# Hybrid encoder layer on one core: the scans of each second head pair and the additions of weight blocks in DRAM placed behind the products of v and z_a, and two of eight pairs of k-tiles, not three, taken as seven products

## The chip, the core and the metric

The kernel runs on one core of a Trainium2 chip. The core has five engines that run side by side, each with its own queue of instructions in a fixed order: PE (matmuls; PEld is its loading of weights), DVE and ACT (elementwise work), POOL (elementwise work, and the DMAs that add) and SP (all other DMAs). The metric is the device time of one execution, in microseconds (us); lower is better.

## The reference

One encoder layer on x of 256 tokens by 2048. After an RMS norm one projection of 2048 x 18432 gives nine blocks of 2048 columns. Five of them (q, v, two forget gates, z_a) feed group A: 16 heads of a gated linear recurrence in chunks of 64 tokens, run forward and backward, summed, normed by head and gated by silu(z_a). The other four feed a short convolution. Both results go through an output projection of 4096 x 2048; an embedding gate and a last norm follow.

```python
hn = _rmsnorm(h, norm_w[i])
proj = hn @ w_in[i]
q, v, f_fwd, f_bwd, z_a, b_gate, c_gate, h_b, z_b = jnp.split(proj, IN_SPLITS, axis=-1)
o_a = _hgrn2_bidirectional(jax.nn.silu(q), v, f_fwd, f_bwd, lb_all[:, i])
o_a = _head_rmsnorm(o_a, hgrn_norm_w[i]) * jax.nn.silu(z_a)
```

Within a chunk the recurrence needs the running sum of log f along the tokens: these running sums are the scans that the change moves.

## The kernel before, in words

**Precision.** Every fp32 weight tile is split into a rounded high part and a low remainder: `Stream.split` casts on ACT (L101) and subtracts on DVE (L102), from `raw` (three buffers of 1 MB, loaded by SP) into `spl` (five buffers). x is split the same way into `xs`. A product of two split matrices is three matmuls (`three`, L523 to L525), or a wide one and a short one where x stands on the right (`gemm_part`, L403 and L401). `Stream.get` keeps the splits three parts ahead of PE.

**Groups.** `two_pairs(i)` handles two head pairs, i and i+1, for i = 0, 2, 4, 6. Each group has two stages. First come the projections: for each of the two pairs, three calls of `gemm_in` (forget forward, forget backward, q), 96 steps of k-tiles in all. Then v and z_a for both pairs at once: `gemm_two` in group 0 and `gemm_vz` in groups 2, 4 and 6. Four convolution projections per channel group follow after the last group, and the output projection after these.

**Seven products.** `gemm_vz` goes through eight pairs of k-tiles (`half`). A plain pair takes eight block products of three matmuls each, 24 matmuls. For a pair in `VZ_SUMS` the 2 x 2 x 2 block product is done with seven products instead of eight, 21 matmuls, at the price of sums: sums of x blocks (`xsums`, once, in group 2, into `xsum`) and sums of weight blocks. The latter are made in DRAM: `prepare` copies two blocks of weights into a tile `vz` (L306, SP), `add_up` adds to them with accumulating DMAs on POOL's queue in three steps (step 0 at L314, steps 1 and 2 at L318), and the result is loaded like a weight tile (`raw<-vz`, L76). A pair with sums splits 3.5 parts, a plain one 2. The banks of the seven products, `ex`, `ey` and two that the scores use as well, are emptied after the last pair with sums (L445 to L449).

**Mixing.** `mix_forgets` (gates, logarithms) and `mix_pair` (scans at L652 and L656, exponentials, the factors `kc`, `qc` and `kx` on POOL at L687 and L693) prepare a pair; `scores` multiplies them on PE (L706, L750), and `outputs` multiplies with v.

**What sets the order.** A counter `tick` runs along with the k-steps of PE. `at(dt, fn)` records the instructions of `fn` when the counter is dt further. A scheduler then places each engine's instructions by its own forecast of readiness; `high_priority` moves an instruction ahead by an offset, and `tc.keep_in_program_order` holds an instruction behind what its engine has been given before. `gemm_vz` counts 49 ticks before the change and 46 after, so a group has 145 or 142. In group 0 the additions come at ticks 98 to 112, during `gemm_two`; in groups 2 and 4 they are for the next group.

Of the kernel before, what the change touches and what calls it, by code (L numbers as in the profile page):

```python
# [12 lines left out]
ALU = mybir.AluOpType  # L13
# [6 lines left out]
T = 256  # L20
# [95 lines left out]
def tile_hymba_encoder(  # L116
# [15 lines left out]
    act, dve, pool, pe = nc.scalar, nc.vector, nc.gpsimd, nc.tensor  # L132
# [16 lines left out]
    ws = Stream(tc, rawp, splp, 3)  # L149


    VZ_ORDER, VZ_SUMS = (0, 1, 2, 3, 4, 6, 5, 7), (2, 4, 6)
    dramp = ctx.enter_context(tc.tile_pool(name="dramp", bufs=1, space=bass.MemoryType.DRAM))
    vz_prepared = {}
    blocks = {}
# [96 lines left out]
    smask = early[:, 0:T]  # L252
# [5 lines left out]
    for j in range(4):  # L258
        sgn = 1 if j < 2 else -1
        pool.affine_select(  # L260
            out=tri[:, j, :], in_=tri[:, j, :], compare_op=ALU.is_ge, fill=0.0, base=0,
# [35 lines left out]
    def at(dt, fn):  # L297
        pend.append((now[0] + dt, len(pend), fn))
# [109 lines left out]
    def gemm_in(c, i, orders={}):  # L408

        acc = acc_in(c, i)  # L410
        for g in range(4):
            gemm_part(acc, ws.get(blocks[c, i][g]), g, orders=orders)
        return acc
# [41 lines left out]
                for m in range(2):  # L455
                    act.activation(dst[:, m], dst[:, m], AF.Copy, scale=rx[:, m : m + 1])

    def evac(acc, dst, tmpp):

        with tc.high_priority(offset=200):  # L460
            for m in range(2):
                r = tmpp.tile([P, T], F32, tag="r", name="r", bufs=2)
                act.copy(out=r, in_=acc[m][:, 1, :])  # L463
                dve.tensor_tensor(out=dst(m), in0=acc[m][:, 0, :], in1=r, op=ALU.add)  # L464
# [8 lines left out]
    acc3 = [acc_in(c, 0) for c in first[:2]]  # L473
# [22 lines left out]
    ap_ = actx.enter_context(tc.tile_pool(name="ap", bufs=1, side="right"))  # L496
# [143 lines left out]
                in1=mixa[:, hd, 0, :], op0=ALU.mult, op1=ALU.subtract,  # L640
            )

    def mix_pair(i, xf, qt, lf):


        pf = ap_.tile([P, 2, 2, T], F32, tag="pf", name=f"pf{i}")
        dd = ap_.tile([P, 2, 2, T], F32, tag="dd", name=f"dd{i}")
        pv = [pf[:, d] for d in range(2)]
        dv = [dd[:, d] for d in range(2)]
        lfl = lf.rearrange("p a b c -> p (a b c)")  # L650
        for h in range(2):
            dve.tensor_tensor_scan(  # L652
                out=pv[0][:, h, :], data0=smask, data1=lf[:, 0, h, :], initial=0.0, op0=ALU.mult, op1=ALU.add
            )
            o = (2 + h) * T - 1
            dve.tensor_tensor_scan(  # L656
                out=pv[1][:, h, :], data0=lfl[:, o : o + T], data1=smask, initial=0.0, op0=ALU.add, op1=ALU.mult
            )
        pf4, pb4, df4, db4 = c64(pv[0]), c64(pv[1]), c64(dv[0]), c64(dv[1])
        lb4 = c64(lf[:, 1])  # L660
        for h in range(2):
            dve.tensor_tensor(
                out=df4[:, h], in0=pf4[:, h], in1=pf4[:, h, :, 31:32].broadcast_to([P, 4, CH]), op=ALU.subtract
# [119 lines left out]
    def two_pairs(i):  # L783
        vt = ap_.tile([P, 2, 512], F32, tag="vt", name=f"vt{i}")
        zt = ap_.tile([P, 2, 512], F32, tag="zt", name=f"zt{i}")
        ss = ap_.tile([P, 2, 2, 2], F32, tag="ss", name=f"ss{i}", bufs=2)
        ogs, steps, forgets = [], [], []
        before = last_two[0]
        if i == 6:
            for z in range(4):  # L790
                at(10 + 10 * z, lambda z=z: prepare(prepared[z]))
        else:


            todo = vz_prepared[i + 2]
            for z, what in enumerate(todo):
                at(50 + 10 * z, lambda what=what: prepare(what))
                for step in range(3):
                    dt = (126 + 10 * z, 160 + 4 * z, 174 + 4 * z)[step] if i else 98 + 6 * step + z
                    at(dt, lambda what=what, step=step: add_up(what, step))  # L800
        if i == 2:

            def xsums(z):
                k = 2 * VZ_SUMS[z]
                a, t = xq[1][:, 0].rearrange("p (k t) -> p k t", k=2), xq[1][:, 1].rearrange("p (o t) -> p o t", o=4)
                act_sums(xs[:, k : k + 2], a, t)
                act_split(xq[0][:, z], xs[:, k : k + 2], t)

            for z in range(len(VZ_SUMS)):
                at(10 + 12 * z, lambda z=z: xsums(z))  # L810
        for e in range(2):
            xf = ap_.tile([P, 2, 2, T], F32, tag="xf", name=f"xf{i + e}", bufs=2)
            qt = ap_.tile([P, 2, T], F32, tag="qt", name=f"qt{i + e}")
            first3 = i + e == 0

            kicks = {(0, 1): ({}, ONE, BOTH), (2, 0): (ONE, BOTH, {}), (4, 0): ({}, {}, BOTH), (6, 0): ({}, {}, BOTH)}
            kick = kicks.get((i, e), ({}, {}, BOTH if i + e else {}))
            for j, (c, dst) in enumerate(((B_FF, xf[:, 0]), (B_FB, xf[:, 1]), (B_Q, qt))):
                evac(acc3[j] if first3 else gemm_in(c, i + e, kick[j]), lambda m, dst=dst: dst[:, m, :], ap_)

            def mix(e=e, xf=xf, qt=qt):
                forgets.append((xf, qt, mix_forgets(i + e, xf, qt)))
                if e == 0:
                    if before:
                        before()
                    steps.append(mix_pair(i, *forgets[0]))

            if first3:

                at(15, mix)  # L830
            else:
                mix()

        def out(e):
            ogs.append(ap_.tile([P, 2, 2, P], F32, tag="ogz", name=f"ogz{i + e}", bufs=2))
            steps[e][1](vt, ogs[e], ss[:, e])

        if i == 0:

            at(18, lambda: steps[0][0]())  # L840
            at(19, lambda: steps.append(mix_pair(i + 1, *forgets[1])))
            at(46, lambda: out(0))
            at(46, lambda: steps[1][0]())
            at(60, lambda: out(1))
            gemm_two(B_V, i, vt)
            xctx.close()
            xqp = xqctx.enter_context(tc.tile_pool(name="xqp", bufs=1, side="left", reuse_waits="tile"))
            xq.append(xqp.tile([P, len(VZ_SUMS), 4, 2, P], F32R, name="xsum"))
            xq.append(xqp.tile([P, 2, 512], F32, name="xd"))
            gemm_two(B_ZA, i, zt)  # L850
        else:

            at(4, lambda: steps[0][0]())
            gemm_vz(i, vt, zt)
            at(8, lambda: steps.append(mix_pair(i + 1, *forgets[1])))
            at(12, lambda: out(0))
            at(32, lambda: steps[1][0]())
            at(42, lambda: out(1))

        def rest():  # L860
            gate_two(i, zt)
            if i < 6:
                at(24, lambda: finish_two(ogs, ss, zt, ogs))
                for e in range(2):
                    at(32, lambda e=e: turn(i + e, ogs[e], "yx"[e]))
            else:

                def keep():
                    kept.extend(psm.tile([P, 2, 2, P], F32, tag=f"sc{e}", name=f"kept{e}") for e in range(2))
                    finish_two(ogs, ss, zt, kept)  # L870

                at(50, keep)

        last_two[0] = rest
# [360 lines left out]
```

## Time and profile before

| | us |
|---|---|
| median of 3 runs | 1152.24 |
| lowest and highest | 1151.96, 1156.35 |
| the profiled execution | 1151.24 |
| its span, first to last instruction | 1149.5 |

The mean granted clock of TensorE is 0.992. Of the profiled time 1.7 us lie around the span. A line of the profile names engine, source line, operation, the tile written and the tiles read. "Idle before, releaser" is how long the engine stood and what let it go on. Windows give the busy time of each engine in a stretch. The matmuls of a row overlap their neighbours, so their pitch, start to start, says what one costs, and not its duration.

### The profile page before, as it was taken

The numbers are of one execution on the slowest core, as the hardware profiler recorded it, in microseconds if no ns is written. First come the engines' busy times: TensorE is split into PE (matmuls) and PEld (weight loads), VectorE is DVE, ScalarE is ACT, GpSimd is POOL, SyncE is SP. The second block draws the span as 40 slices with busy tenths as digits, with TensorE's granted clock in tenths as the row PEclk, the third lists the DMA queues.
The fourth block names the chain that finished last, engine by engine and source line by source line (L and its number), as shares of the span: only waits on it lengthen the run. The fifth ranks groups of instructions, "written<-read, shape, count | busy, mean of one in ns | idle before, by whom it ended". The sixth has DMA issues, their size and how long they took to land.

```text
span 1149.5 us, 17024 instructions
## 1 busy us (share of the span) xinstructions
PE 1114.5 (97%) x6455; PEld 950.8 (83%) x6455; DVE 829.3 (72%) x1100; ACT 677.6 (59%) x947; POOL 300.3 (26%) x251
## 2 busy tenths in 40 slices
PE   9999999789996999999999999999999999999996
PEld 8888888668884888778888888888888888888886
DVE  7899477765784767976657776774767879878573
ACT  6786568445974568755644544544546665565563
POOL 1135324601263016403323413323423000000011
PEclk9999999989999999999999999999999999999999
DMA  9776994997659965487899998999998988887531
GB/s 352 269 251 216 243 298 166 201 288 242 199 156 253 341 212 174 149 277 212 234 302 276 267 297 267 261 295 292 278 257 249 355 278 288 306 295 268 202 128 74
DMA packets 86082, 286.42 MB, mean 249 GB/s; under 512 B 8304, under 2 KB 29424, under 8 KB 67312
## 3 DMA queue, kind: packets, MB, share of 16 engines
q1 hardware_dynamic: 69264, 258.76, 64.6%
q0 software_dynamic: 16448, 26.22, 15.2%
q8 instruction: 51, 0.84, 0.3%
q10 hardware_dynamic: 288, 0.34, 0.1%
q14 instruction: 31, 0.25, 0.1%
HBM read 283.20 MB, written 54.53 MB: 294 GB/s over the span
## 4 chain that ended last, share of the span: by engine, by line
PE 70%; DVE 11%; DMA 6%; POOL 6%; ACT 4%; issue 2%; SPq 0%; DVEq 0%; ACTq 0%; POOLq 0%
PE a L403 28%; PE a L401 14%; DVE spl L102 4%; DMA raw<-in_w_in_dram 4%; PE pg L996 3%; PE pg L997 3%; PE pg L995 3%; DMA raw<-vz 2%; PE pa L523 2%; PE pa L524 2%; PE pa L525 2%; ACT spl L101 2%; POOL kc L687 2%; DVE pf L652 1%; POOL qc L687 1%
## 5 line engine op out<-in xcount | busy, mean ns | idle before, releaser
L102 DVE TENSOR_TENSOR spl<-raw,spl 128x1024 fp32r<-128x1024 f32 (+2 forms) x419 | 503.7, 1215 | 225.9 <-ACT spl L101 223.1
L403 PE MATMUL a<-xs,spl 128*128 128x512 f32 x1792 | 622.8, 393 | 0.4 <-DVE xs L344 0.2
L101 ACT CAST spl<-raw 128x1024 fp32r<-128x1024 f32 (+2 forms) x419 | 413.1, 998 | 263.1 <-PE a L401 89.2
L401 PE MATMUL a<-xs,spl 128*128 128x256 f32 x1792 | 496.3, 279 | 0.0
L403 PEld LDWEIGHTS a<-xs,spl 128*128 128x128 f32 x1792 | 334.3, 187 | 74.8 <-issue 0.6
L401 PEld LDWEIGHTS a<-xs,spl 128*128 128x128 f32 x1792 | 337.4, 189 | 2.1
L1112 POOL TENSOR_TENSOR hh<-hh,fw 128x512 f32<-128x512 f32 (+1 forms) x9 | 11.0, 1226 | 250.7 <-ACT gt L1111 248.1
L463 ACT COPY r<-a 128x256 f32<-128x256 f32 x112 | 40.3, 367 | 37.9 <-PE a L401 37.7
L524 PE MATMUL avz<-spl,xs 128*128 128x512 f32 x138 | 55.4, 401 | 4.9 <-DVE spl L102 4.8
L523 PE MATMUL avz<-spl,xs 128*128 128x512 f32 x138 | 55.3, 401 | 1.2 <-DVE qt L464 1.2
L525 PE MATMUL avz<-spl,xs 128*128 128x512 f32 x138 | 54.5, 395 | 0.0
L995 PE MATMUL pg<-spl,ht 128*128 128x512 f32 (+1 forms) x120 | 45.2, 377 | 0.0
L996 PE MATMUL pg<-spl,ht 128*128 128x512 f32 (+1 forms) x120 | 45.1, 376 | 0.0
L997 PE MATMUL pg<-spl,ht 128*128 128x512 f32 (+1 forms) x120 | 45.0, 375 | 0.0
L755 POOL TENSOR_TENSOR s<-early 128x256 f32<-128x256 f32 x16 | 16.3, 1028 | 105.4 <-DVE early L754 105.4
L101 ACT CAST spl<-early 128x1024 fp32r<-128x1024 f32 (+1 forms) x29 | 28.7, 990 | 19.0 <-PE pb_y L525 7.5
L102 DVE TENSOR_TENSOR spl<-early,spl 128x1024 fp32r<-128x1024 f32 (+1 forms) x29 | 32.8, 1147 | 9.6 <-ACT spl L101 9.1
L468 POOL TENSOR_TENSOR xf<-xf,rbc 128x1024 f32<-128x1024 f32 x8 | 20.8, 2602 | 68.7 <-DVE rbc L379 49.3
L524 PEld LDWEIGHTS avz<-spl,xs 128*128 128x128 f32 x138 | 26.5, 192 | 12.8 <-DVE spl L102 7.5
L912 POOL TENSOR_TENSOR cg<-cg,hb 128x512 f32<-128x512 f32 x8 | 14.8, 1854 | 82.1 <-DVE hb L464 82.1
L523 PE MATMUL pa<-spl,mixa 128*128 128x512 f32 x88 | 34.5, 392 | 0.0
L525 PE MATMUL pa<-spl,mixa 128*128 128x512 f32 x88 | 34.3, 390 | 0.0
(322 smaller groups left out, 1685.5 us busy)
## 6 DMA issues: line engine op xcount, KB each, us to landing
raw<-in_w_in_dram SPq DMA_DIRECT2D x106, 1024.0 KB, 7.4
raw<-in_w_in_dram SPq DMA_DIRECT2D x82, 256.0 KB, 4.4
raw<-in_w_out_dram SPq DMA_DIRECT2D x36, 512.0 KB, 5.2
sums<-in_w_out_dram SPq DMA_DIRECT2D x32, 512.0 KB, 11.0
raw<-in_w_in_dram SPq DMA_DIRECT2D x26, 512.0 KB, 6.6
raw<-sums SPq DMA_DIRECT2D x13, 1024.0 KB, 5.5
vz<-in_w_in_dram SPq DMA_DIRECT2D x36, 256.0 KB, 6.9
raw<-vz SPq DMA_DIRECT2D x9, 1024.0 KB, 7.4
```

What stands on the lines that cost most here:

```text
L101: self.nc.scalar.copy(out=v[:, :, 0], in_=r)
L102: self.nc.vector.tensor_tensor(out=v[:, :, 1], in0=r, in1=v[:, :, 0], op=ALU.subtract)
L401: pe.matmul(a[:, :T], lhsT=lhsT, rhs=xs[:, kt, 0, :], start=False, stop=(kt == NKT - 1))
L403: pe.matmul(a, lhsT=lhsT, rhs=xs[:, kt, :, :].rearrange("p s n -> p (s n)"), start=(kt == 0), stop=False)
L463: act.copy(out=r, in_=acc[m][:, 1, :])
L523: pe.matmul(acc, lhsT=ah, rhs=w[:, 0], start=start, stop=False)
L524: pe.matmul(acc, lhsT=ah, rhs=w[:, 1], start=False, stop=False)
L525: pe.matmul(acc, lhsT=al, rhs=w[:, 0], start=False, stop=stop)
L687: pool.tensor_tensor(out=c64(dst[:, d]), in0=c64(src[:, d, :, half * P : (half + 1) * P]), in1=g.unsqueeze(3).broadcast_to([P, 2, 2, CH]), ...
L995: pe.matmul(acc[m], lhsT=lh, rhs=wh, start=(kt == 0), stop=False)
L996: pe.matmul(acc[m], lhsT=lh, rhs=wl, start=False, stop=False)
L997: pe.matmul(acc[m], lhsT=ll, rhs=wh, start=False, stop=(kt == nk - 1))
```

## The change

Five edits:

- `VZ_SUMS` goes from (2, 4, 6) to (2, 5) and the pairs run in plain order: two pairs of k-tiles with sums in each `gemm_vz`, with pairs 3 and 4 between them.
- The additions for the next group get later due times: steps at 166, 196 and 220 ticks from the start of the group, that is 24, 54 and 78 ticks into the next group's projections. Group 0 keeps its times.
- `mix_pair(i + 1)` of groups 2, 4 and 6 comes 4 ticks after `gemm_vz`, not 8, and its four scans are kept in program order.
- The eviction of the second pair's q has priority offset 500, not 200.
- `out(1)` comes at tick 46, not 42.

```diff
-    VZ_ORDER, VZ_SUMS = (0, 1, 2, 3, 4, 6, 5, 7), (2, 4, 6)
+    VZ_ORDER, VZ_SUMS = range(8), (2, 5)
...
-    def evac(acc, dst, tmpp):
+    def evac(acc, dst, tmpp, offset=200):
-        with tc.high_priority(offset=200):
+        with tc.high_priority(offset=offset):
...
-    def mix_pair(i, xf, qt, lf):
+    def mix_pair(i, xf, qt, lf, here=False):
+        place = tc.keep_in_program_order if here else lambda instr: instr
...
-            dve.tensor_tensor_scan(
-                out=pv[0][:, h, :], data0=smask, data1=lf[:, 0, h, :], initial=0.0, op0=ALU.mult, op1=ALU.add
+            place(
+                dve.tensor_tensor_scan(
+                    out=pv[0][:, h, :], data0=smask, data1=lf[:, 0, h, :], initial=0.0, op0=ALU.mult, op1=ALU.add
+                )
             )
...
-                    dt = (126 + 10 * z, 160 + 4 * z, 174 + 4 * z)[step] if i else 98 + 6 * step + z
+                    dt = (166, 196, 220)[step] + z if i else 98 + 6 * step + z
...
-                evac(acc3[j] if first3 else gemm_in(c, i + e, kick[j]), lambda m, dst=dst: dst[:, m, :], ap_)
+                acc, offset = acc3[j] if first3 else gemm_in(c, i + e, kick[j]), 500 if e and j == 2 else 200
+                evac(acc, lambda m, dst=dst: dst[:, m, :], ap_, offset)
...
-            at(8, lambda: steps.append(mix_pair(i + 1, *forgets[1])))
+            at(4, lambda: steps.append(mix_pair(i + 1, *forgets[1], here=True)))
...
-            at(42, lambda: out(1))
+            at(46, lambda: out(1))
```

What stands where on the engines follows from the scheduler. Before, DVE in group 2: the scores of pair 2 are taken over (L754), and at once, within `gemm_vz`, come the scans of pair 3 (shown as SCALAR_TENSOR_TENSOR at L652 and L656) and what is made of them, with the splits (L102) of the first pair of k-tiles with sums between and behind.

```order
L754 COPY_PREDICATED early<-early,scps_173 128x512
L754 COPY_PREDICATED early<-early,scps_174 128x512
L652 SCALAR_TENSOR_TENSOR pf_2447<-early,lf_2023 128x256
L656 SCALAR_TENSOR_TENSOR pf_2447<-lf_2023,early 128x256
L652 SCALAR_TENSOR_TENSOR pf_2447<-early,lf_2023 128x256
L656 SCALAR_TENSOR_TENSOR pf_2447<-lf_2023,early 128x256
L662 TENSOR_TENSOR dd_2448<-pf_2447 128x256
L665 TENSOR_TENSOR dd_2448<-pf_2447 128x256
L662 TENSOR_TENSOR dd_2448<-pf_2447 128x256
L102 TENSOR_TENSOR spl_2123<-raw_2045,spl_2123 128x512
L665 TENSOR_TENSOR dd_2448<-pf_2447 128x256
L671 TENSOR_TENSOR gx<-dd_2448,pf_2447 128x2x3
```

After the change, the same place (lines of the changed kernel: L759 was L754, L654 and L660 are the scans). The splits follow the scores; the scans stand after the sums that finish v and z_a (L453) and a split of the next group's weights.

```order
L759 COPY_PREDICATED early<-early,scps_170 128x512
L759 COPY_PREDICATED early<-early,scps_171 128x512
L102 TENSOR_TENSOR spl_2101<-raw_2023,spl_2101 128x512
L102 TENSOR_TENSOR spl_2118<-raw_2116,spl_2118 128x2x512
L102 TENSOR_TENSOR spl_2135<-raw_2116,spl_2135 128x2x512
...
L453 TENSOR_TENSOR zt_1353<-avz_3_2013,zt_1353 128x512
L102 TENSOR_TENSOR spl_2424<-raw_2422,spl_2424 128x4x256
L654 SCALAR_TENSOR_TENSOR pf_2391<-early,lf_2001 128x256
L660 SCALAR_TENSOR_TENSOR pf_2391<-lf_2001,early 128x256
L654 SCALAR_TENSOR_TENSOR pf_2391<-early,lf_2001 128x256
L102 TENSOR_TENSOR spl_2445<-raw_2422,spl_2445 128x4x256
```

The scans and all that hangs on them have moved out of `gemm_vz` into the next projections. On POOL, before, group 2: the additions for group 4 follow the scores' sums (L755), within `gemm_vz`; the factors of pair 3 (L687, L693) stand behind the first two additions of step 1.

```order
L755 TENSOR_TENSOR s_2104<-early 128x256 x2
L314 DMA vz_2_84<-in_w_in_dram 256x1x256
L593 TENSOR_TENSOR qt_1706<-qt_1706,sq_2020 128x512
L314 DMA vz_2_84<-in_w_in_dram 256x1x256
L314 DMA vz_4_85<-in_w_in_dram 256x1x256 x2
L314 DMA vz_6_86<-in_w_in_dram 256x1x256 x2
L318 DMA vz_2_84<-vz_2_84 128x512
L318 DMA vz_4_85<-vz_4_85 128x512
L687 TENSOR_TENSOR qc_2471<-pf_2447,ge_2457 128x256
L687 TENSOR_TENSOR kc_2470<-dd_2448,ge_2457 128x256 x2
L693 TENSOR_TENSOR kx_2476<-kc_2470,ge_2457 128x512
```

After the change, the same engine from the factors of pair 3 on (L692, L698), which is in the projections of group 4. Step 0 follows `kx` of pair 3, step 1 the sums of its scores (L760), and step 2 `kx` of pair 4, the last row of factors ahead of `gemm_vz` of group 4.

```order
L698 TENSOR_TENSOR kx_2420<-kc_2414,ge_2401 128x512
L314 DMA vz_2_83<-in_w_in_dram 256x1x256 x2
L314 DMA vz_5_84<-in_w_in_dram 256x1x256 x2
L760 TENSOR_TENSOR s_2636<-early 128x256
...
L760 TENSOR_TENSOR s_2636<-early 128x256
L318 DMA vz_2_83<-vz_2_83 128x512
L318 DMA vz_5_84<-vz_5_84 128x512
...
L698 TENSOR_TENSOR kx_2805<-kc_2799,ge_2786 128x512
L318 DMA vz_2_83<-vz_2_83 128x512
L318 DMA vz_5_84<-vz_5_84 128x512
```

The additions have left `gemm_vz` of groups 2 and 4, but step 2 now comes just ahead of the `gemm_vz` that uses its result.

More of the change, by code (lines that the diff above doesn't have):

```diff
@@ L651, in mix_pair @@
         for h in range(2):
-            dve.tensor_tensor_scan(
-                out=pv[0][:, h, :], data0=smask, data1=lf[:, 0, h, :], initial=0.0, op0=ALU.mult, op1=ALU.add
+            place(
+                dve.tensor_tensor_scan(
+                    out=pv[0][:, h, :], data0=smask, data1=lf[:, 0, h, :], initial=0.0, op0=ALU.mult, op1=ALU.add
+                )
             )
             o = (2 + h) * T - 1
-            dve.tensor_tensor_scan(
-                out=pv[1][:, h, :], data0=lfl[:, o : o + T], data1=smask, initial=0.0, op0=ALU.add, op1=ALU.mult
+            place(
+                dve.tensor_tensor_scan(
+                    out=pv[1][:, h, :], data0=lfl[:, o : o + T], data1=smask, initial=0.0, op0=ALU.add, op1=ALU.mult
+                )
             )
```

## The prediction

> **What bounds the kernel now.** I read the page's busy shares first, then the waits of PE, then windows over the stages.
>
> ```profile
> span 1149.5 us, 17024 instructions
> PE 1114.5 (97%) x6455; PEld 950.8 (83%) x6455; DVE 829.3 (72%) x1100; ACT 677.6 (59%) x947; POOL 300.3 (26%) x251
> ...
> PE ey L523 <- ACT spl L101: 9.8, 5, 3.1
> PE avz L524 <- DVE spl L102: 5.0, 6, 2.0
> PE ey L524 <- DVE spl L102: 3.8, 5, 0.8
> PE ex L524 <- DVE spl L102: 3.2, 3, 1.4
> PE avz L523 <- DVE qt L464: 1.2, 1, 1.2
> ```
>
> PE is the bound, and what it waits for (total us, times, longest) lies almost wholly in one routine: `avz`, `ex` and `ey` are written only where v and z_a are multiplied, and these rows add up to 23.0 us. The windows below hold one line per stretch: its length, then busy time of PE, PEld, DVE, ACT and POOL, the granted clock, the DMA share and GB/s. First the three products of v and z_a (groups 2, 4 and 6), then the projections ahead of the first two.
>
> ```profile
> 195.36:256.63 61.27, 50.71 (x273) 37.70 (x272) 42.57 (x52) 31.21 (x40) 20.05 (x21) 0.94 0.85 219
> 330.27:389.76 59.49, 49.65 (x273) 38.04 (x272) 40.82 (x51) 29.82 (x39) 19.10 (x21) 0.94 0.90 245
> 463.64:512.06 48.42, 45.00 (x274) 36.05 (x272) 41.61 (x51) 29.42 (x39) 13.37 (x12) 1.00 0.66 222
> ...
> 127.84:195.36 67.52, 67.52 (x394) 59.13 (x392) 45.99 (x65) 46.74 (x63) 24.53 (x15) 1.00 0.86 257
> 256.63:330.27 73.64, 73.64 (x513) 65.01 (x513) 50.13 (x73) 56.06 (x85) 23.03 (x13) 1.00 0.65 215
> ```
>
> The projections leave PE no idle time. The three products issue the same matmuls, yet take 61.27, 59.49 and 48.42 us. What the third lacks is the additions in DRAM for a next group: it is a control inside the trace. A stretch of group 4 shows what a wait does on PE (start, duration, idle before):
>
> ```profile
> 369.37 0.39 PE L524 MATMUL avz<-spl,xsum 128*128 128x512 f32 x1
> 369.59 0.39 PE L525 MATMUL avz<-spl,xsum 128*128 128x512 f32 x1
> 373.10 0.50 PE L523 MATMUL ey<-spl,xsum 128*128 128x512 f32 x1 [3.12 <-ACT spl L101]
> ...
> 375.38 0.63 PE L523 MATMUL scps<-spl,xsum 128*128 128x512 f32 x1
> 375.81 0.63 PE L524 MATMUL scps<-spl,xsum 128*128 128x512 f32 x1
> ```
>
> A matmul of 512 columns starts 0.22 to 0.23 us after the one before; after this wait of 3.12 us the pitch is 0.43. So a wait can cost more than itself, and the granted clock of 0.94 in the first two windows is the same thing.
>
> **The change part by part.**
>
> *One pair of k-tiles more as plain products.* 24 matmuls instead of 21, in three groups: 9 x 0.23 = **+2.1 us** on PE, which has no cover.
>
> *The additions move.* Before, POOL's rows of them lie inside the group's v and z_a; now the first addition stands behind `kx` of the group's second head pair and the last behind `kx` of the next group's first pair, in the projections. From the first two windows go at most (61.27 - 48.42) + (59.49 - 48.42) = **-23.9 us**, if they become like the third. The 1.2 us for `qt` are part of that: only the first window has this wait, and the new offset of 500 puts that eviction a split earlier. The additions must not hold up the projections instead. The trace has a stretch of projections with additions landing:
>
> ```profile
> 127.00:152.00 25.00, 25.00 (x144) 21.83 (x143) 12.49 (x14) 13.28 (x17) 3.26 (x4) 1.00 1.09 280
> ```
>
> DMA is at 1.09 there and PE is busy 25.00 of 25.00 us. I take 0 for the new place.
>
> *The scans move.* The third window's own idle time has two sources:
>
> ```profile
> 470.05 1.23 DVE L652 TENSOR_TENSOR_SCAN pf<-early,lf 128x256 f32<-128x256 f32 x1
> ...
> 482.43 3.63 DVE L102 TENSOR_TENSOR spl<-raw,spl 128x1024 fp32r<-128x1024 f32 x2
> ...
> 481.70 0.39 PE L523 MATMUL avz<-spl,xs 128*128 128x512 f32 x1
> 484.12 0.50 PE L524 MATMUL avz<-spl,xs 128*128 128x512 f32 x1 [2.03 <-DVE spl L102]
> ...
> 496.06 0.39 PE L525 MATMUL avz<-spl,xsum 128*128 128x512 f32 x1
> 496.88 0.50 PE L523 MATMUL ey<-spl,xsum 128*128 128x512 f32 x1 [0.43 <-ACT spl L101]
> 498.14 0.50 PE L524 MATMUL ey<-spl,xsum 128*128 128x512 f32 x1 [0.76 <-DVE spl L102]
> ```
>
> From 470.05 to 482.43 DVE works off the second head pair's mixing, and a split that PE wants comes late: start to start 2.42 us instead of 0.23. Then two pairs of k-tiles with sums follow each other (4, 6), and ACT and DVE fall behind: (0.82 - 0.23) + (1.26 - 0.23) = 1.6 us. The scans now stand behind v and z_a, and pairs 2 and 5 are never neighbours. Together 2.2 + 1.6 = 3.8 us. I take 3.0 of it as gone, since splits still share DVE with scores and evictions; the same order stands in all three windows, so 3 x 3.0 = **-9.0 us** (between 0 and -11.4).
>
> *What is late next: the second head pair's scores.* Its scans, and all its mixing behind them, now wait for v and z_a. The third window gives the chain's length, since no addition stands in POOL's way there:
>
> ```profile
> 259.88 0.68 DVE L453 TENSOR_TENSOR zt<-avz,zt 128x512 f32<-128x512 f32 x1
> 260.48 1.21 DVE L102 TENSOR_TENSOR spl<-raw,spl 128x1024 fp32r<-128x1024 f32 x1
> ...
> 484.94 1.60 POOL L687 TENSOR_TENSOR qc<-pf,ge 128x256 f32<-128x256 f32 x1
> ...
> 280.88 0.30 PE L706 MATMUL scps<-qc,dd 128*32 128x128 f32 x2
> ...
> 315.80 5.02 POOL L687 TENSOR_TENSOR kc<-dd,ge 128x256 f32<-128x256 f32 x1 [3.65 <-DVE dd L678]
> ```
>
> From the first scan to the end of the last `qc` it is 486.54 - 470.05 = 16.5 us. The order puts the scans behind the last sum of v and z_a and one split, which end 261.69 - 256.63 = 5.1 us into the next projection. So the factors are there 21.6 us in. PE takes the scores up 280.88 - 256.63 = 24.2 us in. The slack is 2.6 us, not much for a chain over three engines: `kc` alone took 5.02 us once, against 1.60 for this `qc`. I put **+2.0 us** for the three places together (0 if the slack holds, 3 x 4 = 12 if POOL is slow each time; nearer to 0, because the measured chain ran while DVE was fuller).
>
> *What is late next: the sums.* The last addition now waits for `kx`, and the load of the sums waits for it on SP's queue, with the weight tiles queued behind it:
>
> ```profile
> 323.03 1.05 POOL L693 TENSOR_TENSOR kx<-kc,ge 128x512 f32<-128x512 f32 x1
> ...
> 327.55 0.33 SPq L76 DMA_DIRECT2D raw<-vz  x1
> ...
> 345.61 0.39 PE L523 MATMUL ey<-spl,xsum 128*128 128x512 f32 x1
> ...
> raw<-vz SPq DMA_DIRECT2D x9, 1024.0 KB, 7.4
> vz<-in_w_in_dram POOLq DMA_DIRECT2D x18, 256.0 KB, 8.5
> vz<-vz POOLq DMA_DIRECT2D x18, 256.0 KB, 9.5
> ...
> DMA to landing us min/median/max: 4.6/7.5/15.9
> ```
>
> `kx` ends at 324.08; with 9.5 us to landing (the last figure of these rows) the sums are whole at 333.6, so their load goes out 6 us later than its 327.55 and lands at 341.0. PE wants the first part of it at 345.61, a cast and a split, some 2.2 us, behind the landing: slack 2.4 us. The tile behind it has a further pair's time. **+1.0 us** for groups 4 and 6 together (0 to 2 x 4).
>
> *At nothing:* one sum's preparation less on SP and DVE in group 2 (its projections have no PE idle), 1.5 splits less per group, `out(1)` four ticks later, since no wait of PE is for it.
>
> Sum against the profiled execution: -23.9 - 9.0 + 2.1 + 2.0 + 1.0 = -27.8. Its time is 1151.24 (span 1149.5), so 1123.4; the median of the runs shown is 1.0 higher, hence **1124 us**.
>
> A rule weighs on the price of new waits. The Trainium skill, "TensorE: Matmul & The Clock Gate", Part 1, says that the clock halves after an idle window of about 3.4 us. By it three waits of 3 us would cost 9. The trace halves the pitch after 3.12 us already and keeps it so for at least 2.7 us, 1.3 us more each: 13. Both are inside my range.
>
> **The rivals.**
>
> *The contention moves along.* The additions take the same DMA time wherever they stand. Their queue took 15.2% of the span for 26.22 MB, and a group's three sums are twelve transfers of 256 KB, 3.1 MB:
>
> ```profile
> q0 software_dynamic: 16448, 26.22, 15.2%
> ```
>
> That is 174.7 x 3.1 / 26.2 = 21 us for three sums, 14 for two; with the projections' 0.65 x 73.64 = 48 us it makes 62 of 73.64, or 0.84. If a projection stalled at that, the 23.9 us would return: 1124 + 24 = 1148, within 0.5% (5.8 us, about what a measurement of this kernel can tell from no change). Against it stands the row at 1.09 without a PE wait. The Trainium skill, "Trainium Kernel Development and Optimization", Key Constraints, says that DMAs issued from SP, ACT and POOL share the same 16 engines and interleave; by that rule the move saves no DMA time, which is this rival.
>
> *The scores wait.* The slack of 2.6 us is overrun at all three places by 4 us: 1124 + 12 - 2 = 1134. For it: the `kc` of 5.02 us. Against it: that one had `gate_two` and the transposes beside it.
>
> *The sums come very late, and it ends slower.* SP stands at the load of the sums with all weight tiles behind it. To be slower by 0.5% each of two groups must lose (1158 - 1124) / 2 = 17 us beyond 2.4 us of slack: a last addition landing 29 us behind `kx`. The longest landing on these tiles is 15.9 us.
>
> *The change does nothing:* excluded for scans and additions, since the order shows both moved.
>
> **How the numbers follow.** Forecast (1115 to 1130): 0.66. Scores or sums late by some us (1130 to 1142): 0.22. Contention moved (1146 to 1158): 0.07. Slower: 0.05. With the whole 11.4 gone and no new wait the sum gives 1119; the floor of 1115 leaves 4 us below that for the scatter of the runs shown (1151.96 to 1156.35). 1138 at the top takes in most of the second case. Faster by over 0.5%: 0.66 + 0.22 = 0.88; within: 0.07; slower: 0.05.
>
> **What would show it.** Right: windows over the three products of about 46 us each at clock 1.00, no waits of PE on `ey`, PE full in the projections. Wrong: idle of PE ahead of the scores or `cx`; a late `raw<-vz` with PE waiting on `spl`; or projections longer by what the products lost.

## The result, and the profile after

| | before | after |
|---|---|---|
| median, four runs each, us | 1154.30 | 1116.69 |
| lowest and highest | 1151.96, 1157.54 | 1115.47, 1120.22 |
| the profiled execution | 1151.24 | 1116.85 |
| its span | 1149.5 | 1115.1 |

The ratio is 0.9677, with a 95% interval of 0.9641 to 0.9714: faster by 38 us by the medians and by 34 by the two profiled executions. The forecast was 1124 us, with a range of 1115 to 1138.

From the page of the changed kernel, the span and the busy shares:

```profile
span 1115.1 us, 16970 instructions
...
PE 1105.0 (99%) x6464; PEld 951.2 (85%) x6464; DVE 826.7 (74%) x1088; ACT 671.6 (60%) x939; POOL 291.5 (26%) x239
```

PE is busy 9.5 us less, although it has nine matmuls more: the matmuls that ran at half speed after a wait are gone. By the granted clock they were some 7 us of it (an estimate: 0.06 of 61.27 and of 59.49 us). The waits of PE (engine, line, waited for, total us, times, longest), all that are left:

```profile
PE wps L242 <- DVE wz L237: 1.1, 1, 1.1
PE avz L523 <- DVE qt L464: 0.6, 1, 0.6
```

Of 23.0 us of waits in v and z_a 0.6 are left, and none is on `ey` or a split. The windows of the changed kernel: v and z_a of group 2, the projections behind them, v and z_a of group 4, projections, v and z_a of group 6.

```profile
194.22:238.79 44.57, 44.57 (x276) 36.98 (x275) 33.22 (x36) 28.18 (x34) 4.54 (x4) 1.00 0.69 231
238.79:312.68 73.89, 73.89 (x514) 65.23 (x513) 58.46 (x86) 54.68 (x85) 35.99 (x26) 1.00 0.74 209
312.68:358.15 45.47, 44.84 (x276) 37.04 (x275) 33.52 (x37) 29.58 (x36) 4.54 (x4) 1.00 0.78 260
358.15:432.04 73.89, 73.89 (x514) 65.21 (x513) 58.49 (x86) 55.58 (x86) 35.93 (x26) 1.00 0.79 234
432.04:476.65 44.61, 44.61 (x276) 37.02 (x275) 33.34 (x36) 28.64 (x35) 6.01 (x7) 1.00 0.77 254
```

Read lengths first: 61.27, 59.49 and 48.42 us have become 44.57, 45.47 and 44.61, at a clock of 1.00. The two projections, which took in the additions and the scans, have PE busy in all of their 73.89 us, as before. DVE is the column that shows the move: 7 to 9 us less in a product, 8 more in the first projection. The span lost 34.4 us, and 16.7 + 14.0 + 3.8 = 34.5 of that lie in the three products. All other stretches together changed by 0.1 net.

The two new risks were the scores of the second head pair and the sums. From the timeline of the changed kernel, group 2's projections start at 238.79 (start, duration):

```profile
241.79 0.68 DVE L654 TENSOR_TENSOR_SCAN pf<-early,lf 128x256 f32<-128x256 f32 x1
242.39 0.66 DVE L660 TENSOR_TENSOR_SCAN pf<-lf,early 128x256 f32<-128x256 f32 x1
...
255.53 1.05 POOL L698 TENSOR_TENSOR kx<-kc,ge 128x512 f32<-128x512 f32 x1
256.53 4.24 POOL L314 DMA_DIRECT2D vz<-in_w_in_dram  x4
...
263.27 0.30 PE L711 MATMUL scps<-qc,dd 128*32 128x128 f32 x2
...
306.63 1.05 POOL L698 TENSOR_TENSOR kx<-kc,ge 128x512 f32<-128x512 f32 x1
307.63 1.67 POOL L318 DMA_DIRECT2D vz<-vz  x2
...
308.10 4.72 DVE L102 TENSOR_TENSOR spl<-raw,spl 128x1024 fp32r<-128x1024 f32 x1 [0.45 <-ACT spl L101]
...
308.72 3.01 POOL L468 TENSOR_TENSOR xf<-xf,rbc 128x1024 f32<-128x1024 f32 x1
...
312.93 0.33 SPq L76 DMA_DIRECT2D raw<-vz  x1
```

The scans start 3.0 us into the projection, the last factor `kx` is done at 256.58, and PE takes the scores up at 263.27: a slack of 6.7 us. The last additions of the sums are issued from 307.63, and their load goes out at 312.93, 5.3 us later. Nobody waits for it. The split on DVE that takes 4.72 us in place of 1.2 is the one cost in sight, and it comes back below.

### The profile page after: what moved, and what is told of

Read it like the earlier page. It is cut to its first block, busy times and chain, and to the rows that moved or that the text cites. A ratio compares the mean times of both kernels' runs of the same rounds, so it can differ in the third digit from the quotient of the medians.

```text
span 1115.1 us, 16970 instructions
## 1 busy us (share of the span) xinstructions
PE 1105.0 (99%) x6464; PEld 951.2 (85%) x6464; DVE 826.7 (74%) x1088; ACT 671.6 (60%) x939; POOL 291.5 (26%) x239
## 4 chain that ended last, share of the span: by engine, by line
PE 94%; ACT 2%; DMA 2%; POOL 1%; DVE 1%; issue 0%; DVEq 0%; ACTq 0%; POOLq 0%
PE a L403 34%; PE a L401 18%; PE avz L523 3%; PE avz L524 3%; PE avz L525 3%; PE pg L1004 3%; PE pg L1003 3%; PE pg L1005 3%; PE pa L523 2%; PE pa L524 2%; PE pa L525 2%; DMA raw<-in_w_in_dram 2%; PE a L424 1%; PE a L422 1%; PE a L423 1%; PE pb_sc L524 1%
## 5 line engine op out<-in xcount | busy, mean ns | idle before, releaser
L102 DVE TENSOR_TENSOR spl<-raw,spl 128x1024 fp32r<-128x1024 f32 (+2 forms) x413 | 505.7, 1238 | 190.1 <-ACT spl L101 187.5
L101 ACT CAST spl<-raw 128x1024 fp32r<-128x1024 f32 (+2 forms) x413 | 409.0, 1001 | 250.6 <-PE a L401 88.1
L523 PE MATMUL avz<-spl,xs 128*128 128x512 f32 x156 | 61.0, 391 | 0.6 <-DVE qt L464 0.6
L525 PE MATMUL avz<-spl,xs 128*128 128x512 f32 x156 | 60.7, 389 | 0.0
L524 PE MATMUL avz<-spl,xs 128*128 128x512 f32 x156 | 60.7, 389 | 0.0
L692 POOL TENSOR_TENSOR qc<-pf,ge 128x256 f32<-128x256 f32 x16 | 23.2, 1453 | 106.5 <-ACT ge L679 95.6
L468 POOL TENSOR_TENSOR xf<-xf,rbc 128x1024 f32<-128x1024 f32 x8 | 22.0, 2750 | 73.4 <-DVE rbc L379 49.4
L102 DVE TENSOR_TENSOR spl<-early,spl 128x1024 fp32r<-128x1024 f32 (+1 forms) x29 | 32.9, 1147 | 9.4 <-ACT spl L101 8.7
L523 PEld LDWEIGHTS avz<-spl,xs 128*128 128x128 f32 x156 | 29.3, 188 | 6.9 <-DVE qt L464 0.8
L523 PE MATMUL pa<-spl,mixa 128*128 128x512 f32 x88 | 34.5, 392 | 0.0
L525 PEld LDWEIGHTS avz<-spl,xs 128*128 128x128 f32 x156 | 29.3, 188 | 6.1
## 6 DMA issues: line engine op xcount, KB each, us to landing
sums<-in_w_out_dram SPq DMA_DIRECT2D x32, 512.0 KB, 11.4
```

Source lines behind the costliest of these rows:

```text
L101: self.nc.scalar.copy(out=v[:, :, 0], in_=r)
L102: self.nc.vector.tensor_tensor(out=v[:, :, 1], in0=r, in1=v[:, :, 0], op=ALU.subtract)
L523: pe.matmul(acc, lhsT=ah, rhs=w[:, 0], start=start, stop=False)
L524: pe.matmul(acc, lhsT=ah, rhs=w[:, 1], start=False, stop=False)
L525: pe.matmul(acc, lhsT=al, rhs=w[:, 0], start=False, stop=stop)
L692: pool.tensor_tensor(out=c64(dst[:, d]), in0=c64(src[:, d, :, half * P : (half + 1) * P]), in1=g.unsqueeze(3).broadcast_to([P, 2, 2, CH]), ...
```

## The experiments

Three theories stood ahead of the runs. **A**: the additions' transfers inside v and z_a are the root, as the third product, which has none, says. **B**: the scans and the late splits behind them are the root. **C**: the number of sums, or two pairs of k-tiles with sums as neighbours, is the root. Each run was timed in three rounds, beside the kernel before in the same rounds. The last column has the lengths of the three products of v and z_a in the profiled execution.

| run | what it is | us | before, us | ratio, 95% interval | products, us |
|---|---|---|---|---|---|
| e1 | before, additions at the new due times | 1150.78 | 1152.84 | 0.998 [0.9969, 0.9992] | 58.14, 57.83, 50.98 |
| e8 | before, all additions out of the products | 1147.81 | 1151.85 | 0.9965 [0.9951, 0.9979] | 50.26, 54.13, 54.69 |
| e2 | before, scans behind | 1137.85 | 1152.84 | 0.9864 [0.9838, 0.989] | 52.43, 52.88, 45.72 |
| e3 | before, two sums (2, 5) | 1131.17 | 1152.84 | 0.9807 [0.9784, 0.9831] | 52.02, 50.28, 46.97 |
| e5 | after, additions at the old due times | 1117.18 | 1152.84 | 0.9684 [0.9661, 0.9706] | 45.89, 44.57, 44.57 |
| e6 | after, scans back | 1129.33 | 1151.85 | 0.9802 [0.9782, 0.9823] | 48.54, 48.72, 48.78 |
| e7 | after, three sums in the old order | 1120.46 | 1151.85 | 0.9721 [0.9701, 0.9741] | 43.90, 49.64, 45.18 |
| e4 | after, three sums (2, 4, 6) in plain order | 1122.35 | 1151.85 | 0.9745 [0.9726, 0.9763] | 43.89, 48.18, 46.30 |
| e11 | before, additions left out | 1129.01 | 1152.47 | 0.9793 [0.9757, 0.9828] | 49.93, 47.93, 48.51 |
| e12 | e7, additions left out | 1116.35 | 1152.47 | 0.9683 [0.965, 0.9716] | 43.89, 43.90, 43.89 |
| e9 | before, three sums (2, 4, 6) in plain order | 1148.93 | 1152.47 | 0.9967 [0.9951, 0.9983] | 59.34, 56.16, 48.31 |
| e10 | before, two sums as neighbours | 1131.99 | 1152.47 | 0.982 [0.979, 0.985] | 53.00, 51.11, 46.47 |

### One part alone: e1, e8, e2, e3

The additions alone, at the due times of the change:

```diff
-                    dt = (126 + 10 * z, 160 + 4 * z, 174 + 4 * z)[step] if i else 98 + 6 * step + z
+                    dt = (166, 196, 220)[step] + z if i else 98 + 6 * step + z
```

> The kernel before with the later due times of the additions alone (three sums, old order of k-tiles, scans as before). Step 0 now stands behind kx of the second head pair, which with the scans as before still lies inside v and z_a; steps 1 and 2 are in the projections. Theory A (the DMA traffic of the additions inside v and z_a costs 23.9 us): half of the traffic is gone or more, so the windows of groups 2 and 4 fall from about 60 to 48-54 us and the time by 12 to 24 us. Theory B (the scans are the root: they delay the splits, the splits free the raw buffers late, and only then do loads and additions collide): under 8 us, windows of 57 us or more. Theory C (the number and neighbourhood of sums is the root): under 5 us.

It gains 2 us. As expected, step 0, six of the twelve additions, stays inside the products (issued from 24.6 and 25.3 us into them), and the other six have left. Theory A priced that at 12 to 24 us, and it missed; theory B, with under 8 us and products of 57 us or more, forecast what came. It is no proof against A, since a new place can have a price of its own, as the next run shows. With later due times all twelve leave:

```diff
-                    dt = (126 + 10 * z, 160 + 4 * z, 174 + 4 * z)[step] if i else 98 + 6 * step + z
+                    dt = (192, 200, 222)[step] + z if i else 98 + 6 * step + z
```

> The kernel before with the additions alone moved so late (192, 200, 222 ticks) that all three steps stand behind the second head pair's scores, in the projections; three sums in the old order, scans as before. Unlike the run with the due times of the change, no addition is left inside v and z_a. Theory A (traffic of the additions inside v and z_a): groups 2 and 4 become like group 6, about 48 to 51 us, the time falls by 17 to 24 us. Theory B (late splits are the root, additions cost little): 57 us or more stay, under 8 us fall. Theory C (the sums, their number and neighbourhood, are the root): under 8 us.

The gain is 4 us, which is not the 17 to 24 of theory A; but the products are not the 57 us of theory B either. Its windows, product of group 2, projections, and so on in turn:

```profile
195.00:245.26 50.26, 46.46 (x274) 37.47 (x272) 43.39 (x53) 31.62 (x41) 11.88 (x9) 0.97 0.62 207
245.26:323.76 78.50, 74.98 (x514) 65.18 (x512) 47.51 (x71) 51.57 (x81) 30.81 (x25) 1.00 0.79 225
323.76:377.89 54.13, 48.51 (x273) 38.55 (x272) 46.87 (x54) 33.84 (x43) 14.34 (x11) 0.94 0.73 233
377.89:453.00 75.11, 74.17 (x513) 65.20 (x512) 47.54 (x71) 51.62 (x81) 30.80 (x25) 1.00 0.81 242
453.00:507.69 54.69, 48.63 (x273) 38.45 (x272) 46.34 (x53) 33.07 (x42) 15.78 (x14) 0.94 0.68 217
```

The first product falls to 50.26, as a place without additions should. But the projections grow by 4.9 and 1.2 us, and the products of groups 4 and 6, which follow them, stand at 54 to 55. The timeline of the same run around the second of these products (start 323.76) shows what comes late:

```profile
298.39 0.81 POOL L318 DMA_DIRECT2D vz<-vz  x1 [6.10 <-DMA vz<-in_w_in_dram]
298.93 1.59 POOL L468 TENSOR_TENSOR qt<-qt,rbc 128x512 f32<-128x512 f32 x1
...
321.31 2.51 POOL L318 DMA_DIRECT2D vz<-vz  x3
...
321.78 5.54 DVE L102 TENSOR_TENSOR spl<-raw,spl 128x1024 fp32r<-128x1024 f32 x1 [0.46 <-ACT spl L101]
...
322.92 3.30 POOL L468 TENSOR_TENSOR xf<-xf,rbc 128x1024 f32<-128x1024 f32 x1
...
327.37 0.50 PE L524 MATMUL avz<-spl,xs 128*128 128x512 f32 x1 [1.83 <-DVE spl L102]
...
334.77 0.76 PE L523 MATMUL avz<-spl,xs 128*128 128x512 f32 x1 [2.08 <-DVE qt L464]
```

POOL stands 6.10 us until a transfer lands, with the normalised q (`qt` on L468) queued behind the addition. At 321.31 it issues the three last additions and starts the next normalisation, and in that time a split on DVE takes 5.54 us. PE then waits for splits and for the eviction of q. So the third product was a true control for the old place of the additions, but the new place has a price of its own: of 23 us 19 come back, 6 in the two projections and 13 in the products.

The scans alone, with the changed kernel's other edits to the mixing; against the changed kernel this is:

```diff
-    VZ_ORDER, VZ_SUMS = range(8), (2, 5)
+    VZ_ORDER, VZ_SUMS = (0, 1, 2, 3, 4, 6, 5, 7), (2, 4, 6)
...
-                    dt = (166, 196, 220)[step] + z if i else 98 + 6 * step + z
+                    dt = (126 + 10 * z, 160 + 4 * z, 174 + 4 * z)[step] if i else 98 + 6 * step + z
```

> The kernel before with the scans of the second head pair behind v and z_a alone (with the eviction offset and the two small shifts that belong to it); additions at the old due times, three sums. Theory A: 2.3 us per group, 7 us in all, groups 2 and 4 still at 55 us or more. Theory B: 25 us or more, groups 2 and 4 at about 47 us. Theory C: under 7 us.

It gains 15 us, and mostly where additions stand: the first two products lose 8.8 and 6.6 us, the third 2.7. That lies between theory A (7 us) and theory B (25 or more).

Two sums instead of three alone:

```diff
-    VZ_ORDER, VZ_SUMS = (0, 1, 2, 3, 4, 6, 5, 7), (2, 4, 6)
+    VZ_ORDER, VZ_SUMS = range(8), (2, 5)
```

> The kernel before with two sums (pairs 2 and 5, plain order) alone; additions and scans as before. Theory A: a third of the additions' 23.9 us and 1.6 us per group for the neighbouring sums, less 2.1 us for the plain pair: about 11 us faster. Theory B: about 3 us. Theory C: 20 us or more.

This part, which I had booked as a cost of 2.1 us, gains 21.7 us by itself. A third of the additions goes with the third sum. The gain is in theory C's range; what the third sum costs is settled further down. Alone the parts give 4, 15 and 22 us, 41 together, while the whole change gives 34 to 38. That is too close to tell much; how far the parts overlap shows when they are taken out of the whole.

### One part undone: e5, e6, e7, e4

The changed kernel with the additions at their old due times:

```diff
-                    dt = (166, 196, 220)[step] + z if i else 98 + 6 * step + z
+                    dt = (126 + 10 * z, 160 + 4 * z, 174 + 4 * z)[step] if i else 98 + 6 * step + z
```

> The changed kernel with the additions back at their old due times, so that they lie inside v and z_a of groups 2 and 4; scans behind, two sums. Theory A: two thirds of 23.9 us come back, about 16 us slower than the changed kernel, all of it in the windows of groups 2 and 4. Theory B: 4 us or less, since the splits now free the raw buffers in time. Theory C: 4 us or less.

It is as fast as the changed kernel. The windows of its products of groups 2 and 4:

```profile
193.15:239.04 45.89, 45.16 (x277) 36.82 (x275) 32.74 (x36) 26.37 (x32) 9.54 (x9) 1.00 0.80 236
312.92:357.49 44.57, 44.57 (x276) 36.97 (x275) 31.34 (x35) 25.64 (x32) 9.66 (x9) 1.00 0.89 271
```

Five of the eight additions are issued inside each product (the scheduler puts the others behind `kx`), the DMA share is 0.89 in the second, and PE is busy in all of its 44.57 us. With two sums and the scans behind, additions inside the product cost 0 to 1.3 us, as theories B and C said. It takes both: e2 has the scans behind too, but three sums and seven of twelve additions inside, and its first two products are 8.5 and 9.0 us longer than the 43.9 of the same kernel without additions (e12). Theory A as the sole root falls here.

The changed kernel with the mixing as before, and the additions late enough to stay out of the products:

```diff
-                    dt = (166, 196, 220)[step] + z if i else 98 + 6 * step + z
+                    dt = (192, 200, 222)[step] + z if i else 98 + 6 * step + z
...
-                acc, offset = acc3[j] if first3 else gemm_in(c, i + e, kick[j]), 500 if e and j == 2 else 200
+                acc, offset = acc3[j] if first3 else gemm_in(c, i + e, kick[j]), 200
...
-            at(4, lambda: steps.append(mix_pair(i + 1, *forgets[1], here=True)))
+            at(8, lambda: steps.append(mix_pair(i + 1, *forgets[1])))
...
-            at(46, lambda: out(1))
+            at(42, lambda: out(1))
```

> The changed kernel (two sums, plain order) with the scans as before and the additions wholly in the projections. Theory A: only the scans' own delay comes back, 2.4 us in each of the three windows (47.0 us each, as the third window of the run with two sums alone), 7 us slower than the changed kernel, about 1124. Theory B: 20 us or more slower. Theory C: under 3 us slower.

All three products are 3.3 to 4.2 us longer than with the scans behind: 11.4 us. No theory had this: A said 7, B 20 or more, C under 3.

The changed kernel with three sums in the old order (e7), and with three in plain order (e4):

```diff
-    VZ_ORDER, VZ_SUMS = range(8), (2, 5)
+    VZ_ORDER, VZ_SUMS = (0, 1, 2, 3, 4, 6, 5, 7), (2, 4, 6)
```

> The changed kernel with three sums in the old order (4 and 6 neighbours), additions and scans as changed. Theory A: all three windows like the third of the run with the scans alone, 45.7 us, so 3 to 4 us slower than the changed kernel, about 1120. Theory B: the same. Theory C: 15 us or more slower, waits of PE on ey and ex back.

```diff
-    VZ_ORDER, VZ_SUMS = range(8), (2, 5)
+    VZ_ORDER, VZ_SUMS = range(8), (2, 4, 6)
```

> The changed kernel with three sums (2, 4, 6) in plain order, so that no two are neighbours. Nine matmuls of 0.23 us less than the changed kernel: 2.1 us faster, about 1114.6, if no wait comes with it (theories A and B). Theory C: slower than the changed kernel by 5 us or more, since a third sum brings DMA and splits that v and z_a have no room for.

Both lie above the changed kernel, e4 clearly, e7 with an interval that overlaps the changed kernel's a little. The windows of e7's first two products:

```profile
195.52:239.42 43.90, 43.90 (x274) 36.40 (x272) 34.37 (x37) 27.99 (x34) 4.54 (x4) 1.00 0.71 233
...
314.52:364.16 49.64, 46.07 (x274) 37.53 (x272) 38.42 (x39) 31.12 (x38) 6.80 (x5) 0.97 0.82 257
```

The third sum saves PE its matmuls, as 43.90 against 44.57 shows, but only in group 2. In group 4 the product is 5.7 us longer, right behind three last additions. For e7 theories A and B had the time (about 1120), but by luck: they had all products at 45.7 us, and 43.90, 49.64 and 45.18 came. For e4 theory C had the loss of 5 us or more. The split that was held for 5.5 us in e8 is here too:

```profile
312.38 5.52 DVE L102 TENSOR_TENSOR spl<-raw,spl 128x1024 fp32r<-128x1024 f32 x1 [0.45 <-ACT spl L101]
...
317.95 0.50 PE L524 MATMUL avz<-spl,xs 128*128 128x512 f32 x1 [1.66 <-DVE spl L102]
```

It starts 2.1 us ahead of the product (314.52), and PE waits 1.66 us for it. In the changed kernel the split of 4.72 us starts 4.6 us ahead (308.10 against 312.68), and PE does not wait for it. By these rows the difference lies more in when that split comes than in its 0.8 us more.

### The additions left out: e11, e12

Both kernels leave out every addition in DRAM, so that the sums stay incomplete; the copies, the loads and all work on PE, ACT and DVE remain. e11 is the kernel before, e12 is e7:

```diff
-                    at(dt, lambda what=what, step=step: add_up(what, step))
+                    if i < 0:
+                        at(dt, lambda what=what, step=step: add_up(what, step))
```

> The kernel before with the additions in DRAM left out altogether (the copies and the loads of the sums stay, so the sums are incomplete); scans and three sums as before. The prediction's term (groups 2 and 4 become like group 6): all three windows at 48 to 49 us, 24 us faster, about 1128. If so, the additions do cost that in their old place, and moving them gave only 4 us because they cost nearly as much in the new one. Rival (late splits and the sums' own load set the windows, the additions little): 55 us or more stay in groups 2 and 4, under 10 us faster.

The products of e11:

```profile
195.59:245.52 49.93, 46.40 (x273) 37.47 (x272) 43.47 (x53) 31.64 (x41) 11.88 (x9) 0.97 0.61 208
319.40:367.33 47.93, 45.87 (x274) 37.47 (x272) 42.21 (x52) 30.14 (x40) 11.89 (x9) 0.96 0.70 242
441.21:489.72 48.51, 44.95 (x273) 36.02 (x272) 41.61 (x51) 29.28 (x39) 13.37 (x12) 1.00 0.65 220
```

This is the control made real: without additions all three are within 1.5 us of the third of before. Their price in the old kernel is 169.18 - 146.37 = 22.8 us. What is left above a full PE belongs to something else.

> The changed kernel with three sums in the old order and the additions left out (the sums are incomplete). With additions this kernel took 1120.5 us, and the windows 43.9, 49.6 and 45.2. If the additions that POOL issues just ahead of v and z_a, with a split beside them that took 5.5 us, are what a third sum fails on: 43.9 us in all windows, about 1113. If the third sum's own loads and splits are: 47 us or more stay in group 4, 1118 or more.

The products of e12:

```profile
198.89:242.78 43.89, 43.89 (x273) 36.41 (x272) 34.70 (x38) 28.35 (x35) 4.55 (x4) 1.00 0.71 237
316.66:360.56 43.90, 43.90 (x274) 36.42 (x273) 32.97 (x37) 27.12 (x33) 4.67 (x4) 1.00 0.77 264
434.44:478.33 43.89, 43.89 (x273) 36.41 (x272) 33.52 (x37) 27.21 (x34) 5.98 (x7) 1.00 0.75 254
```

PE is full in all three, with the neighbours 4 and 6 in place. So the scans' place is worth 146.37 - 131.68 = 14.7 us with three sums, and neither the number nor the neighbourhood of the sums costs PE anything where no additions run. Against e7 it shows that the 5.7 us of group 4 are the additions' too. (The forecast of 43.9 us in all windows came true, that of 1113 us did not: its stretch ahead of group 2 took 3.4 us longer than e7's, which hides part of the gain in the whole time.)

### Neighbours: e9, e10

The kernel before with three sums in plain order, and with two that are neighbours:

```diff
-    VZ_ORDER, VZ_SUMS = (0, 1, 2, 3, 4, 6, 5, 7), (2, 4, 6)
+    VZ_ORDER, VZ_SUMS = range(8), (2, 4, 6)
```

> The kernel before with three sums (2, 4, 6) in plain order, so that none are neighbours; scans and additions as before. If the neighbourhood of 4 and 6 is what two sums took away: 12 us or more faster than before. If it is the number of sums: under 4 us.

```diff
-    VZ_ORDER, VZ_SUMS = (0, 1, 2, 3, 4, 6, 5, 7), (2, 4, 6)
+    VZ_ORDER, VZ_SUMS = (0, 1, 2, 3, 5, 4, 6, 7), (3, 5)
```

> The kernel before with two sums that are neighbours (pairs 3 and 5, order 0 1 2 3 5 4 6 7); scans and additions as before. If the number of sums is what counts: like the run with two sums apart, 1128 to 1134. If the neighbourhood is: 1140 or more.

Separating three sums gives 3.5 us. Putting two side by side costs nothing against e3: 0.982 [0.979, 0.985] beside 0.9807 [0.9784, 0.9831]. The neighbourhood is not the root; theory C is left with the number alone, and, with the scans behind, that works through the additions: without them three sums cost nothing (e12).

No run is faster than the changed kernel beyond the intervals. e5 and e12 equal it, and e12 leaves work out.

## Why the prediction held, and where its steps did not

The time lies in the range, but near its lower end, and by some luck: the prediction's own bounds, with the whole 11.4 us gone and no new wait, end at 1119 us, and 1116.69 lies inside only by the 4 us left for scatter. What was to show it right does: products of 44.6 to 45.5 us, a clock of 1.00, no wait on `ey`, full projections. The terms, with e11 and e12 as steps between before and after (one order of taking them; as steps from before to after they must add up to the whole):

| term | predicted | measured | from |
|---|---|---|---|
| additions leave the products | -23.9 | -22.8 | before to e11 |
| scans behind, sums apart | -9.0 | -14.7 | e11 to e12 |
| one plain pair more, three groups | +2.1 | +2.0 | e12's 43.89 to 44.57, three times |
| additions in their new place | 0 | +0.9 | 45.47 in group 4 against 44.57 |
| scores late | +2.0 | 0 | no wait of PE, slack 6.7 us |
| sums late | +1.0 | 0 | no wait of PE |
| sum | -27.8 | -34.6 | the span changed by -34.4 |

- **Additions.** "It is a control inside the trace" was right, to 1.1 us. But it priced the old place only, with the scans and three sums in place. The changed kernel does not need the move: e5 leaves the additions at their old due times, five of eight inside the products, and is as fast. So these 23.9 us can be had without the move, by the scans and two sums.
- **"I take 0 for the new place"** failed as a rule, and held here by the size of the change. With two sums, POOL issues two last additions ahead of v and z_a, and the cost is the 0.64 us wait on `qt` and little more. With three sums the same move returns 19 of 23 us in the kernel before (e8) and, with the scans behind, 5.7 us in group 4 (e7). The row that I argued from had DMA at 1.09 and PE full, and it answered the wrong question: what returns goes with POOL's order and a split held on DVE, while the DMA share is only 0.79 in e8's projections. For the held split the rows speak for POOL: its input was there (ACT's cast of it released it), and it is longer by just the time that POOL takes to issue the additions (last section). POOL's own wait of 6.10 us is for a transfer, and for the rest of the loss no run parts POOL's order from the traffic. The rival "the contention moves along" is therefore out for this change, but not for e8, where most of the time did return, by these rows through another mechanism.
- **Scans.** The failed step is "Together 2.2 + 1.6 = 3.8 us. I take 3.0 of it as gone", with a bound of 11.4 for all three. It took the third product as the floor but for two places with visible gaps. Its distance to a full PE is 48.42 - 43.89 = 4.5 us, and all of that went; group 2 without additions stood 6.0 above. The neighbourhood of pairs 4 and 6, named as the cause of 1.6 us of it, costs nothing once the scans are behind and no additions run (e12): their late splits hung on these. With two sums the scans' place is worth 11.4 us (e6), with three 14.7.
- **Plain pair.** The pitch of 0.22 to 0.23 gave 2.1; 3 x 0.68 = 2.0 was measured.
- **Scores and sums.** Both slacks were read too short. The scans start 3.0 us into the projection, not 5.1, and run 0.66 to 0.68 us each while POOL stands idle (the first one shown in the prediction took 1.23, beside a sum on POOL), so the chain ends 17.8 us in and not 21.6. The load of the sums went out 5.3 us after the issue of the last addition, not 9.5 behind `kx`. The half pitch after a wait of 3.12 us had no wait to act on. So the changed kernel does not test the rule of the Trainium skill, "TensorE: Matmul & The Clock Gate", Part 1, on an idle window of about 3.4 us. But e8 does, and it does not agree: no wait of PE in its second product is longer than 2.08 us, and the granted clock there is 0.94.
- **The parts as separate terms.** The sum came out 6.8 us short: the scans' term was 5.7 us too small and 3.0 us of new waits did not come, while 2 us at the additions went the other way. The parts are not separate: each alone gives another number: moving the additions is worth 4 us in the kernel before (e8), about 17 once the scans are behind (e2 to e7), and nothing measurable with two sums (e5). Two sums, booked as a pure cost, carry most of the gain when alone (e3).

One correction to the text ahead of the prediction: a plain pair counts 8 ticks in `gemm_vz`, not 4, so this stage counts 61 before and 62 after, and the new due times are 8, 38 and 62 ticks into the next group's projections. The prediction took the places from the order, so no term rests on it.

Open: whether three sums would win with their last additions elsewhere in the projections was not tried. The new offset of the eviction and the two small shifts were never run apart from the scans.

## What to carry to other kernels

A stretch that lacks one suspect gives the price of that suspect in its old place, and no price for the new one: look at what the engine that issues the moved work does next, and who shares its inputs. A control is not a floor; measure a stage against its own full engine, its matmuls at their undisturbed pitch, before bounding what a change can give. Where several edits relieve the same wait, take one away from the whole as well as adding one alone, for each alone may look like most of the gain, or like none of it.

## What the runs showed of the hardware

A split on DVE does not share time with POOL's large tensor operations: the one that comes second ends behind the other. From the timeline of the kernel before, POOL's normalisation (L468) and the split beside it, at two places:

```profile
189.90 3.38 POOL L468 TENSOR_TENSOR xf<-xf,rbc 128x1024 f32<-128x1024 f32 x1
...
324.04 2.40 POOL L468 TENSOR_TENSOR xf<-xf,rbc 128x1024 f32<-128x1024 f32 x1
...
189.77 1.25 DVE L102 TENSOR_TENSOR spl<-raw,spl 128x1024 fp32r<-128x1024 f32 x1 [0.45 <-ACT spl L101]
...
324.49 3.03 DVE L102 TENSOR_TENSOR spl<-raw,spl 128x1024 fp32r<-128x1024 f32 x1 [0.46 <-ACT spl L101]
```

At 189.77 the split came 0.13 us first: it kept its 1.25 us, and POOL took 3.38 in place of 2.40. At 324.49 POOL came first, and the split ended at 327.52, 1.08 us after POOL's instruction, which is nearly its whole length. In the changed kernel it ends at 312.82, POOL at 311.73; in e8 at 327.32 and 326.22. That is 1.09 and 1.10 us, whether the split was recorded with 3.03, 4.72 or 5.54. The Trainium skill, "SBUF — State Buffer", "Who interferes with whom", says that a DVE instruction with two SBUF inputs contends with a GpSimd instruction that reads SBUF, and that the order of issue decides who waits; these rows agree. What they add is the case with additions: there the split started 0.62 and 1.14 us ahead of POOL's normalisation and was held all the same, while POOL was still issuing the additions.

The issue alone does not hold a split. In the kernel before, in group 2, POOL issues five additions in a row, and the splits beside them keep their length:

```profile
207.06 5.77 POOL L314 DMA_DIRECT2D vz<-in_w_in_dram  x5
...
210.92 1.22 DVE L102 TENSOR_TENSOR spl<-raw,spl 128x1024 fp32r<-128x1024 f32 x1
...
212.75 1.23 DVE L102 TENSOR_TENSOR spl<-raw,spl 128x1024 fp32r<-128x1024 f32 x1
```

A split beside two additions at L318 kept it too (1.23 us at 134.69). By these rows it is the normalisation right behind the additions that holds the split. The held split took 3.03 us with no addition ahead, 4.72 with two and 5.54 with three. That is 1.69 and 2.51 us more, and POOL issued the two in 1.67 us and the three in 2.51. So in these three places the split waits out the issue and the normalisation. It is no general rule: in e5 a split that came while one addition was issued, with the scores' sum (L760) behind that, kept 1.22 us (at 383.57). Why the others were held before the normalisation ran, the rows do not tell.
